# Instance normalisation on one core: transfers moved from SyncE's hardware queue to GpSimd's software queue

## The chip, the core and the metric

The kernel runs on one core of one Trainium2 chip. The core has a vector engine (VectorE, DVE in the profile), a scalar engine (ScalarE, ACT), GpSimd (POOL), SyncE (SP), a matrix engine that is not used here, and 16 DMA engines that move data between the chip's main memory and the on-chip memory SBUF. The metric is the device time in microseconds; less is better. The kernel before takes 4962.8 us, the median of five runs (4962.3 to 4964.85).

## What is computed

Every row of 4096 numbers is normalised by itself. There are 256 x 256 = 65536 rows of float32.

```
batch = 256
channels = 256
length = 4096
def reference(x: np.ndarray, eps: np.float32) -> np.ndarray:
    mean = np.mean(x, axis=2, keepdims=True)
    var = np.var(x, axis=2, keepdims=True)
    return ((x - mean) / np.sqrt(var + eps)).astype(np.float32)
```

1.07 GB are read and 1.07 GB are written.

## The kernel before

A tile is 128 partitions of 4 rows each, 512 rows or 8.39 MB; there are 128 tiles. A partition's four rows lie next to each other in memory, 64 KB in one piece. SBUF holds three such tiles, X[0] to X[2], and tile t lives in X[t % 3]; the load, the computation and the store all work in place in it.

VectorE does two passes over each row. L87 sums it (a tensor_scalar with an accumulator). ScalarE then squares the centred row with an accumulator (L137) and takes a root per pair of rows (L146). VectorE makes the reciprocal and the bias (L98, L100) and applies them (L112, a tensor_scalar without an accumulator). Of the last row of a tile, ScalarE applies the first 3072 elements (L151) and VectorE the rest.

The first and the last tile are worked in two halves of two rows each, each with its own store; the first tile is also loaded in two halves.

All transfers are issued by SyncE from one program (L196 to L218). In the middle, a loop of 41 rounds over three tiles (L208) does the same for each tile t: wait until tile t is done (L164), issue its store (L165), wait until the store of tile t-1 has landed, since tile t+2 goes into its buffer (L169), issue the load of tile t+2 (L170). The transfers of one queue start in the order of issue. So the data moves as store t, load t+2, store t+1, load t+3. At the end, after the loop has stored tile 124 and loaded tile 126, SyncE issues load 127 (L212), then store 125, store 126 and the two half stores of tile 127 (L213 to L216).

Each landing is a semaphore: loaded[s] and stored[s], one per buffer and a fourth for the second halves, each raised by 16 by one transfer. The function take (L66) waits for a value and clears the semaphore. VectorE waits for loaded itself, at the start of a tile (L85). The semaphore done[s] counts the five writes that finish a tile. GpSimd does nothing in the kernel's body.

Of the kernel before, what the change touches and what calls it, by code (L numbers as in the profile page):

```python
# [10 lines left out]
def kernel(  # L11
# [6 lines left out]
    nc = tc.nc  # L18
# [5 lines left out]
    K = 4  # L24
    BUFS = 3
# [4 lines left out]
    n, d = x_flat.shape  # L30
    assert n % (P * K) == 0 and d & (d - 1) == 0

    ntiles = n // (P * K)
    x_t = x_flat.rearrange("(t p k) d -> t p k d", p=P, k=K)
    out_t = out_flat.rearrange("(t p k) d -> t p k d", p=P, k=K)
    assert ntiles == 128

    half = K // 2
# [8 lines left out]
    X = [pool.tile([P, K, d], fp32, name=f"x{s}") for s in range(BUFS)]  # L47
# [5 lines left out]

    loaded = [nc.alloc_semaphore(f"loaded{s}") for s in range(BUFS + 1)]
    stored = [nc.alloc_semaphore(f"stored{s}") for s in range(BUFS + 1)]
    own_v = nc.alloc_semaphore("own_v")
# [3 lines left out]
    scaled = nc.alloc_semaphore("scaled")  # L62
    done = [nc.alloc_semaphore(f"done{s}") for s in range(BUFS + 1)]
    ready = nc.alloc_semaphore("ready")

    def take(engine, sem, count):  # L66
        engine.wait_ge(sem, count)  # L67
        engine.sem_clear(sem)  # L68

    V, A, S = nc.vector, nc.scalar, nc.sync  # L70

    def vector_tile(s, r0=0, k=K, ld=None, dn=None):

        x = X[s]
        ld = loaded[s] if ld is None else ld
        dn = done[s] if dn is None else dn
        own = 0

        def mine(instruction):
            nonlocal own  # L80
            own += 1
            return instruction.then_inc(own_v, 1)

        if ld:
            take(V, ld, 16)  # L85
        for r in range(r0, r0 + k):
            V.tensor_scalar(  # L87
                out=x[:, r, :], in0=x[:, r, :], scalar1=1.0 / d, scalar2=None, op0=ALU.mult, op1=ALU.add,
                accum_out=mean[s][:, r : r + 1],
            ).then_inc(means, 1)  # L90
        for b in range(r0, r0 + k, 2):
            c = slice(b, b + 2)
            final = b == r0 + k - 2
            if final:
                take(V, stds, (b - r0) // 2 + 1)
            else:
                V.wait_ge(stds, (b - r0) // 2 + 1)
            mine(V.reciprocal(out=rstd[s][:, c], in_=std[s][:, c]))  # L98
            V.wait_ge(own_v, own)
            mine(V.scalar_tensor_tensor(  # L100
                out=nbias[s][:, c], in0=mean[s][:, c], scalar=-1.0 / d, in1=rstd[s][:, c], op0=ALU.mult, op1=ALU.mult
            ))
            if final:
                take(V, own_v, own)
            else:
                V.wait_ge(own_v, own)
            if final:
                V.sem_inc(scaled, 1)
            for r in range(b, b + 2):
                c = slice(r, r + 1)  # L110
                f = slice(Q, d) if r == r0 + k - 1 else slice(0, d)
                V.tensor_scalar(  # L112
                    out=x[:, r, f], in0=x[:, r, f], scalar1=rstd[s][:, c], scalar2=nbias[s][:, c],
                    op0=ALU.mult, op1=ALU.add,
                ).then_inc(dn, 1)

    def scalar_tile(s, r0=0, k=K, ld=None, dn=None):

        x = X[s]
        dn = done[s] if dn is None else dn  # L120
        last = r0 + k - 1
        own = 0

        def mine(instruction):
            nonlocal own
            own += 1
            return instruction.then_inc(own_a, 1)

        for r in range(r0, last + 1):
            c = slice(r, r + 1)  # L130
            if own:
                A.wait_ge(own_a, own)
            if r == last:
                take(A, means, k)
            else:
                A.wait_ge(means, r - r0 + 1)
            mine(A.activation(  # L137
                out=junk, in_=x[:, r, :], func=AF.Square, bias=mean[s][:, c], scale=-float(d), accum_out=ss[s][:, c]
            ))
            if (r - r0) % 2:  # L140
                c = slice(r - 1, r + 1)
                if r == last:
                    take(A, own_a, own)
                else:
                    A.wait_ge(own_a, own)
                A.activation(  # L146
                    out=std[s][:, c], in_=ss[s][:, c], func=AF.Sqrt, bias=eps_tile, scale=1.0 / d**3
                ).then_inc(stds, 1)
        c = slice(last, last + 1)
        take(A, scaled, 1)  # L150
        A.activation(  # L151
            out=x[:, last, :Q], in_=x[:, last, :Q], func=AF.Identity, bias=nbias[s][:, c], scale=rstd[s][:, c]
        ).then_inc(dn, 1)

    def rows_of(ap, t):

        if isinstance(t, int):
            return ap[t]
        first, period, count, i = t
        ap = ap[first : first + period * (count - 1) + 1 : period]  # L160
        return ap[bass.ds(i, 1)].rearrange("o p k d -> p (o k) d")

    def store(s, t):
        take(S, done[s], K + 1)  # L164
        S.dma_start(out=rows_of(out_t, t), in_=X[s][:, :, :]).then_inc(stored[s], 16)  # L165

    def load(s, t, wait=True):
        if wait:
            take(S, stored[s], 16)  # L169
        S.dma_start(out=X[s][:, :, :], in_=rows_of(x_t, t)).then_inc(loaded[s], 16)  # L170

    def half_of(h):
        return slice(h * half, (h + 1) * half)

    def second(sems, s, h):
        return sems[BUFS] if h else sems[s]

    def store_half(s, t, h):
        r = half_of(h)
        take(S, second(done, s, h), half + 1)  # L180
        S.dma_start(out=out_t[t][:, r, :], in_=X[s][:, r, :]).then_inc(second(stored, s, h), 16)

    def halves(tile_fn, s, first):
        for h in range(2):
            ld = second(loaded, s, h) if first or h == 0 else False
            tile_fn(s, h * half, half, ld, second(done, s, h))

    last = ntiles - 1
    rounds = (ntiles - 5) // BUFS
    L0 = 2  # L190

    with tc.tile_critical():  # L192
        with nc.Block() as block:  # L193

            @block.sync
            def _(sync):  # L196
                for h in range(2):
                    r = half_of(h)
                    S.dma_start(out=X[0][:, r, :], in_=x_t[0][:, r, :]).then_inc(second(loaded, 0, h), 16)
                load(1, 1, wait=False)  # L200
                store_half(0, 0, 0)
                store_half(0, 0, 1)
                load(2, 2, wait=False)
                store(1, 1)
                take(S, stored[BUFS], 16)
                load(0, 3)

                with S.Fori(0, rounds) as i:  # L208
                    for t in range(L0, L0 + BUFS):
                        store(t % BUFS, (t, BUFS, rounds, i))  # L210
                        load((t + 2) % BUFS, (t + 2, BUFS, rounds, i))
                load(last % BUFS, last)  # L212
                store((last - 2) % BUFS, last - 2)  # L213
                store((last - 1) % BUFS, last - 1)
                store_half(last % BUFS, last, 0)
                store_half(last % BUFS, last, 1)  # L216
                for s in ((last - 2) % BUFS, (last - 1) % BUFS, last % BUFS, BUFS):
                    take(S, stored[s], 16)  # L218

            @block.vector  # L220
            def _(vector):
                V.memset(eps_tile, eps / d**2).then_inc(ready, 1)  # L222
                halves(vector_tile, 0, True)
                vector_tile(1)
                with V.Fori(0, rounds) as i:  # L225
                    for j in range(BUFS):
                        vector_tile((L0 + j) % BUFS)
                vector_tile((last - 2) % BUFS)
                vector_tile((last - 1) % BUFS)
                halves(vector_tile, last % BUFS, False)  # L230

            @block.scalar
            def _(scalar):
                take(A, ready, 1)
                halves(scalar_tile, 0, True)
                scalar_tile(1)
                with A.Fori(0, rounds) as i:
                    for j in range(BUFS):
                        scalar_tile((L0 + j) % BUFS)
                scalar_tile((last - 2) % BUFS)  # L240
                scalar_tile((last - 1) % BUFS)
                halves(scalar_tile, last % BUFS, False)
# [35 lines left out]
```

## Time and profile before

| what | value |
|---|---|
| median of five runs | 4962.8 us |
| profiled execution, its time | 4963.14 us |
| its span, first to last instruction | 4960.9 us |
| VectorE busy | 3298.2 us, 66% |
| ScalarE busy | 2407.6 us, 49% |
| L87, one row, 128x4096 | 4416 ns, 512 times |
| L112, one row, 128x4096 | 2411 ns, 382 times |
| L137, one row, 128x4096 | 3678 ns, 512 times |
| HBM read and written | 1073.74 MB each |

The span is the stretch that the profile covers; the time of the same execution has some 2.2 us more around it. Busy times are sums over instructions of one engine and may lie beside each other. In the row of 40 slices that the page has for the DMA engines each digit is the busy share of a slice in tenths. In a timeline each line has a start and a duration in microseconds, the engine, the line of the kernel, the operation and what it writes and reads; the bracket gives how long the engine was idle before it and what ended that. "SPq" is SyncE's sequencer, where transfers are issued. A DMA issue's last number is the median time from issue to landing.

### The profile page before, as it was taken

Reading aid. Unit: us, or ns where it says so; the run is one execution under the profiler, and the core shown is the slowest. Engines: PE = TensorE matmul, PEld = TensorE weight load, DVE = VectorE, ACT = ScalarE, POOL = GpSimd, SP = SyncE. Lnnn points to the kernel's source line nnn. Section 1 sums busy time; section 2 is a strip of 40 time slices with the busy share of each in tenths; the row PEclk is TensorE's granted clock in tenths of the full one; section 3 lists DMA queues with packets and bytes.
Section 4 is the critical chain, followed back from the end, with each engine's and each line's share of the span. In section 5 each row is a group of like instructions: output and inputs, shape, how many; then the busy total and the mean of one; then the engine's idle time right before and its main releaser. Section 6 shows DMA issues by size and latency. Waiting matters only on the chain.

```text
span 4960.9 us, 5954 instructions
## 1 busy us (share of the span) xinstructions
DVE 3298.2 (66%) x2049; ACT 2407.6 (49%) x1412; POOL 0.2 (0%) x4
## 2 busy tenths in 40 slices
DVE  6666666666666666666666666666666666666666
ACT  4455444554445544455445544455444554445544
POOL 0000000000000000000000000000000000000000
DMA  9999999999999999999999999999999999999999
GB/s 423 431 435 432 433 433 435 432 434 436 432 435 433 434 432 435 433 432 433 434 434 433 435 433 434 436 431 435 435 432 435 435 432 435 434 433 437 432 435 409
DMA packets 37298, 2147.52 MB, mean 433 GB/s; under 512 B 4144, under 2 KB 4144, under 8 KB 4144
## 3 DMA queue, kind: packets, MB, share of 16 engines
q1 hardware_dynamic: 37296, 2147.50, 100.0%
q14 instruction: 2, 0.02, 0.0%
HBM read 1073.74 MB, written 1073.74 MB: 433 GB/s over the span
## 4 chain that ended last, share of the span: by engine, by line
DVE 62%; another core or an unknown queue 31%; issue 4%; DMA 2%; ACT 0%; DVEq 0%; ACTq 0%; SPq 0%
DVE x L87 44%; DVE x L112 16%; DMA x<-in_x_dram 1%; DVE nbias L100 1%; DMA out_dram<-x 1%; DVE rstd L98 1%; ACT junk L137 0%; DVEq L68 0%; DVEq L225 0%; ACT L146 0%; ACT std L146 0%; DVEq L193 0%; ACTq L68 0%; ACTq L67 0%
## 5 line engine op out<-in xcount | busy, mean ns | idle before, releaser
L87 DVE TENSOR_SCALAR_CACHE_REDUCE x<-x 128x4096 f32<-128x4096 f32 x512 | 2232.3, 4416 | 1580.7 <-DMA x<-in_x_dram 1580.7
L137 ACT ACTIVATE junk<-x,mean 128x4096 f32<-128x4096 f32 x512 | 1883.1, 3678 | 2367.5 <-DVE x L87 2367.5
L112 DVE TENSOR_SCALAR x<-x,rstd,nbias 128x4096 f32<-128x4096 f32 (+1 forms) x512 | 1004.3, 2004 | 33.9 <-DVE nbias L100 29.3
L151 ACT ACTIVATE x<-x,nbias,rstd 128x3072 f32<-128x3072 f32 x130 | 383.2, 2947 | 146.3 <-DVEq L68 146.3
L137 ACT ACTIVATION_READ_ACCUMULATOR junk<-x,mean 128x1 f32 x512 | 95.5, 186 | 0.0
L146 ACT ACTIVATE std<-ss,eps_tile 128x2 f32<-128x2 f32 x256 | 75.6, 295 | 19.1
L98 DVE RECIPROCAL rstd<-std 128x2 f32<-128x2 f32 x256 | 40.8, 159 | 19.4 <-ACT std L146 19.4
L100 DVE SCALAR_TENSOR_TENSOR nbias<-mean,rstd 128x2 f32<-128x2 f32 x256 | 41.2, 161 | 8.9
L87 DVE DVE_READ_ACCUMULATOR x<-x 128x1 f32 x512 | 42.4, 83 | 0.0
L137 ACT ACT_TABLE_LOAD x1 | 1.3, 1283 | 1.2 <-DVE eps_tile L222 1.2
L146 ACT ACT_TABLE_LOAD x1 | 1.3, 1283 | 0.1
L222 DVE MEMSET eps_tile<- 128x1 f32 x1 | 0.1, 59 | 1.0 <-SPq L192 1.0
L259 POOL MEMSET const-bfloat16-1.0<- 128x1 bf16 x1 | 0.1, 101 | 0.0
L259 POOL MEMSET const-uint8-127<- 128x1 uint8 x1 | 0.1, 101 | 0.0
L259 POOL MEMSET const-float32-0.0<- 128x1 f32 x1 | 0.1, 98 | 0.2 <-issue 0.2
L259 POOL MEMSET const-float32-1.0<- 128x1 f32 x1 | 0.1, 98 | 0.0
## 6 DMA issues: line engine op xcount, KB each, us to landing
out_dram<-x SPq DMA_DIRECT2D x4, 4096.0 KB, 19.5
x<-in_x_dram SPq DMA_DIRECT2D x2, 4096.0 KB, 16.8
x<-in_x_dram SPq DMA_DIRECT2D x127, 50.3
out_dram<-x SPq DMA_DIRECT2D x126, 31.6
```

Source lines behind the costliest of these rows:

```text
L87: V.tensor_scalar(out=x[:, r, :], in0=x[:, r, :], scalar1=1.0 / d, scalar2=None, op0=ALU.mult, op1=ALU.add, accum_out=mean[s][:, r : r + 1 ...
L98: mine(V.reciprocal(out=rstd[s][:, c], in_=std[s][:, c]))
L100: mine(V.scalar_tensor_tensor(out=nbias[s][:, c], in0=mean[s][:, c], scalar=-1.0 / d, in1=rstd[s][:, c], op0=ALU.mult, op1=ALU.mult))
L112: V.tensor_scalar(out=x[:, r, f], in0=x[:, r, f], scalar1=rstd[s][:, c], scalar2=nbias[s][:, c], op0=ALU.mult, op1=ALU.add,).then_inc(dn, 1)
L137: mine(A.activation(out=junk, in_=x[:, r, :], func=AF.Square, bias=mean[s][:, c], scale=-float(d), accum_out=ss[s][:, c]))
L146: A.activation(out=std[s][:, c], in_=ss[s][:, c], func=AF.Sqrt, bias=eps_tile, scale=1.0 / d**3).then_inc(stds, 1)
L151: A.activation(out=x[:, last, :Q], in_=x[:, last, :Q], func=AF.Identity, bias=nbias[s][:, c], scale=rstd[s][:, c]).then_inc(dn, 1)
L222: V.memset(eps_tile, eps / d**2).then_inc(ready, 1)
L259: nc = _bacc.Bacc("TRN2", target_bir_lowering=False, num_devices=1)
```

## The change

All transfers are issued by GpSimd instead of SyncE, so they go to the software queue[...]. The loop is written out: 128 tiles, one after the other. VectorE doesn't wait for a load's own semaphore any more: GpSimd waits for it and raises a new semaphore, landed[0] (or landed[1] for second halves of the first tile), by one, and VectorE takes that. The semaphores loaded and stored are not cleared; they count up, and GpSimd keeps the value that is due.

The order in the middle is the same, with the new wait for the load of tile t+1 after the issue of load t+2. At the start load 2 is issued before the stores of tile 0. At the end load 127 is issued after store 125.

```diff
-    V, A, S = nc.vector, nc.scalar, nc.sync
+    V, A, S = nc.vector, nc.scalar, nc.gpsimd
...
-        if ld:
-            take(V, ld, 16)
+        if ld is not False:
+            take(V, landed[0] if ld is None else ld, 1)
...
+    due = {}
+
+    def transfer(out, in_, sem):
+        due[sem.name] = due.get(sem.name, 0) + 16
+        S.dma_start(out=out, in_=in_).then_inc(sem, 16)
+
+    def wait(sem):
+        S.wait_ge(sem, due[sem.name])
...
+    def load(t, h=None):
+        s = t % BUFS
+        r = slice(0, K) if h is None else half_of(h)
+        transfer(X[s][:, r, :], x_t[t][:, r, :], second(loaded, s, h))
+
+    def store(t, h=None):
+        s = t % BUFS
+        r = slice(0, K) if h is None else half_of(h)
+        take(S, second(done, s, h), (K if h is None else half) + 1)
+        transfer(out_t[t][:, r, :], X[s][:, r, :], second(stored, s, h))
+
+    def tell(t, h=None):
+        wait(second(loaded, t % BUFS, h))
+        S.sem_inc(landed[1] if h else landed[0], 1)
...
-            @block.sync
-            def _(sync):
...
-                with S.Fori(0, rounds) as i:
-                    for t in range(L0, L0 + BUFS):
-                        store(t % BUFS, (t, BUFS, rounds, i))
-                        load((t + 2) % BUFS, (t + 2, BUFS, rounds, i))
-                load(last % BUFS, last)
-                store((last - 2) % BUFS, last - 2)
-                store((last - 1) % BUFS, last - 1)
-                store_half(last % BUFS, last, 0)
-                store_half(last % BUFS, last, 1)
...
+            @block.gpsimd
+            def _(gpsimd):
+                load(0, 0)
+                load(0, 1)
+                load(1)
+                load(2)
+                tell(0, 0)
+                tell(0, 1)
+                store(0, 0)
+                store(0, 1)
+                tell(1)
+                for t in range(1, ntiles - 2):
+                    store(t)
+                    wait(stored[(t - 1) % BUFS])
+                    if t == 1:
+                        wait(stored[BUFS])
+                    load(t + 2)
+                    tell(t + 1)
+                store(last - 1)
+                tell(last)
+                store(last, 0)
+                store(last, 1)
+                for s in range(BUFS + 1):
+                    wait(stored[s])
```

More of the change, by code (lines that the diff above doesn't have):

```diff
@@ L64 @@
     ready = nc.alloc_semaphore("ready")
+    landed = [nc.alloc_semaphore(f"landed{h}") for h in range(2)]
     def take(engine, sem, count):
@@ L68, in take @@
         engine.sem_clear(sem)
-    V, A, S = nc.vector, nc.scalar, nc.sync
+    V, A, S = nc.vector, nc.scalar, nc.gpsimd
     def vector_tile(s, r0=0, k=K, ld=None, dn=None):
         x = X[s]
-        ld = loaded[s] if ld is None else ld
         dn = done[s] if dn is None else dn
@@ L153, in scalar_tile @@
         ).then_inc(dn, 1)
[L155 to L170, printed above, removed]
+    due = {}
[4 more added lines that the diff above has]
+        S.wait_ge(sem, due[sem.name])
     def half_of(h):
@@ L176, in second @@
         return sems[BUFS] if h else sems[s]
[L178 to L181, printed above, removed]
+    def load(t, h=None):
[10 more added lines that the diff above has]
+        S.sem_inc(landed[1] if h else landed[0], 1)
     def halves(tile_fn, s, first):
         for h in range(2):
-            ld = second(loaded, s, h) if first or h == 0 else False
+            ld = landed[h] if first or h == 0 else False
             tile_fn(s, h * half, half, ld, second(done, s, h))
@@ L193 @@
         with nc.Block() as block:
-            @block.sync
-            def _(sync):
[L197 to L206, printed above, removed]
-                with S.Fori(0, rounds) as i:
-                    for t in range(L0, L0 + BUFS):
-                        store(t % BUFS, (t, BUFS, rounds, i))
-                        load((t + 2) % BUFS, (t + 2, BUFS, rounds, i))
-                load(last % BUFS, last)
-                store((last - 2) % BUFS, last - 2)
-                store((last - 1) % BUFS, last - 1)
-                store_half(last % BUFS, last, 0)
-                store_half(last % BUFS, last, 1)
-                for s in ((last - 2) % BUFS, (last - 1) % BUFS, last % BUFS, BUFS):
-                    take(S, stored[s], 16)
+            @block.gpsimd
[22 more added lines that the diff above has]
+                    wait(stored[s])
             @block.vector
```

## The prediction

> **What bounds the kernel now.** I read the page first: busy row, the row of DMA shares, the queue rows, the DMA issues. Then the waits, the timeline of one tile in the middle, and the timeline of the end; and the landing events and packet records of the trace for single times.
>
> ```profile
> span 4960.9 us, 5954 instructions
> DVE 3298.2 (66%) x2049; ACT 2407.6 (49%) x1412; POOL 0.2 (0%) x4
> DMA  9999999999999999999999999999999999999999
> DMA packets 37298, 2147.52 MB, mean 433 GB/s; under 512 B 4144, under 2 KB 4144, under 8 KB 4144
> q1 hardware_dynamic: 37296, 2147.50, 100.0%
> ...
> out_dram<-x SPq DMA_DIRECT2D x4, 4096.0 KB, 19.5
> x<-in_x_dram SPq DMA_DIRECT2D x2, 4096.0 KB, 16.8
> x<-in_x_dram SPq DMA_DIRECT2D x127, 50.3
> out_dram<-x SPq DMA_DIRECT2D x126, 31.6
> ```
>
> The 16 DMA engines are full in every slice, DVE idles for a third. One tile is 8.39 MB each way, 19.3 us at 434 GB/s; load plus store is 38.6 us, and 128 of these are 4945 us of the 4960.9. The median store lands 31.6 us after its issue, of which 19.3 is its own movement: it stands in the queue for 12.3 us before its turn. That is the slack of the middle. The waits say the same from DVE's side, and the timeline of a middle tile shows it:
>
> ```profile
> DVE x L87 <- DMA x<-in_x_dram: 1580.7, 126, 13.9
> ```
>
> ```profile
> 2434.28 0.34 SPq L165 DMA_DIRECT2D out_dram<-x  x1
> 2434.86 0.35 SPq L170 DMA_DIRECT2D x<-in_x_dram  x1
> 2446.50 4.42 DVE L87 TENSOR_SCALAR_CACHE_REDUCE x<-x 128x4096 f32<-128x4096 f32 x1 [12.46 <-DMA x<-in_x_dram]
> ```
>
> Tile t is done and both its store and the load of t+2 are issued at 2434.9; the load in progress lands only at 2446.4. DVE does nothing in those 12 us.
>
> At the end the last tile's two half stores are still covered by work queued ahead of them:
>
> ```profile
> 4882.17 4.42 DVE L87 TENSOR_SCALAR_CACHE_REDUCE x<-x 128x4096 f32<-128x4096 f32 x1 [12.64 <-DMA x<-in_x_dram]
> ...
> 4908.16 4.41 DVE L87 TENSOR_SCALAR_CACHE_REDUCE x<-x 128x4096 f32<-128x4096 f32 x1
> ...
> 4925.21 17.21 SPq L181 DMA_DIRECT2D out_dram<-x  x2
> ```
>
> Tile 126 lands at 4882.0 and starts at 4882.17; tile 127 starts at 4908.16 without a wait, so it had landed (4901.4 by the trace's landing events). Its half stores go out at 4925.21 and 4942.1 (25.21+17.21 less one issue of 0.34); the last landing is 4959.6, and the span ends 1.4 later.
>
> **What the Trainium skill says.** (1) "DMA: Bandwidth & Descriptors", The descriptor swizzle: a software transfer over 128 partitions makes 9 read and 9 write descriptors per engine, 8 of data and one of completion. The hardware queue here has the same cut: 259 transfers x 16 x 9 = 37296 packets, the very count of the profile's page. (2) Same page, Specifications: first byte about 1 us on the software path, about 0.6 on the hardware one. Here the first issue is at 0.96 and the first data packets start at 2.0, so 1.0 on the hardware path; the software path is not in this trace. (3) "SBUF — State Buffer", Who interferes with whom: a tensor_scalar that doesn't write its accumulator can take both SBUF ports and shuts GpSimd out from writing descriptors until it ends. The trace agrees as to which form is the fast one: L112 takes 2411 ns for 4096 elements, L87 with accumulator 4416. No run here shows the shutting out. (4) Same DMA page, Anatomy of one DMA: the software path fits 2.0 us + bytes/436e3, so its steady rate equals what I see here (434 GB/s).
>
> **The change part by part.** Sums stand against the profiled execution: span 4960.9, time 4963.14, 2.2 us around it; the median of the runs is 4962.8, so I carry the difference over to that.
>
> *Middle, 123 tiles.* Order on the queue: store t, load t+2, as before. New on POOL: a wait for the landing of t+1 and a semaphore increment before the next store. Queued behind that wait is only store t+1, which needs tile t+1 computed and so landed anyway: no cost. The relay puts perhaps 0.1 to 0.3 us (two semaphore steps; DVE here starts 0.15 us after a landing) before DVE's start, and the store's descriptors are later by the software path's delay. Both come out of the 12.3 us slack. Even 3 us per issue would fit. DVE's fast form runs in the microseconds before done, and DVE is idle from done to the next landing, just where both issues fall; so the lock of (3) has nothing to hold up. Cost 0 while issue to first byte stays under some 12 us; past that each microsecond costs 126.
>
> *Rate of the stream.* The trace's packet records give 2418 ns for 65536 bytes and 1213 for 32768: 1205 ns per 32 KB and 8 ns fixed per packet. Each engine moves 2048 rows, 2048 x 2418 = 4952 us: the whole span. So 1 ns more per row is 2 us. By (1) and (4) I take the same packets and the same rate: 0. Bounds: below, all 8 ns fixed gone, -16.4; above, rows cut in two +16.4, in four +49, in sixteen +246 (8 ns for each extra piece).
>
> *Head.* Before: first issue 0.96, first bytes 2.0. POOL does four memsets by 0.44 and starts with the block like SP. Taken +0.8 (skill: +0.4; up to 3 for the first software issue). Load 2 now stands before the stores of tile 0: the same bytes in another order; four issues stand before the first tell, and half 0's landing at 12.7 leaves them 11 us. Tile 2 is told only after load 3 is issued, which waits for the stores of tile 0 (landing 62.4+19.3 = 81.7). Then landing-to-issue as in the middle (2407.7 to 2434.3, 26.6) gives its store at 108.5, its turn is at about 120: 0.
>
> *Tail.* This is a part of the diff that isn't about the queue. Before: load 127 was queued ahead of store 125. After: store 125, load 127, store 126, halves. The bytes are the same, but load 127 lands one store later: 4901.4+19.4 = 4920.8. DVE starts at 4920.8+0.15+0.2 = 4921.1, 12.95 later than 4908.16. The half stores go out at 4938.2 and 4942.1+12.95 = 4955.05. The queue ends store 126 at 4940.2 and the first half at 4949.9: the first half is just in time, the second finds the engines dry for 5 us. An issue to empty engines lands after 12.1 us (the least of the page's load halves, 0.96 to 13.1), with the software path 12.9: 4968.0, against 4959.6. So +8.4. Bounds: +7.6 with no software delay, +11 with 3 us of it (the first half late too).
>
> *Instruction fetch.* POOL's program is unrolled over 125 tiles instead of looped: some 80 KB instead of the 20 KB of queue q14, at 27 GB/s of one engine 2 to 3 us on that engine if all fall on one. The engines end 6.4 us apart (4953.2 to 4959.6 in the last landing), so only the slowest counts. Taken +0.8, bounds 0 to 3.
>
> *End.* POOL waits for the four stored semaphores as SP did: 0, bound +2 for closing the software queue.
>
> Sum: 0.8 + 8.4 + 0.8 = +10.0, and about 1 for the unknown closing: 4962.8 + 11 = 4974.
>
> **The rivals.** A change under 0.2% (9.9 us) can't be told from none here.
> A, forecast: the middle and the rate as before, head and tail as above, +8 to +17; 4974, own range 4969 to 4982. For it: 12.3 us slack, same packet cut. Against: no software transfer is in the trace.
> B: the software ring costs per row, by smaller pieces or by one engine that the ring slows down. 4974+16 = 4990 for one cut, 5023 for four pieces, 5220 for sixteen. For it: a saturated stream hides nothing. Against: the page's 9 descriptors and 436 GB/s.
> C: generation is slower than the slack, for instance held up by DVE. At 15 us it is 3 x 126 = 380 us, 5350. Against it: DVE idle at both issues.
> D, other side: not slower. The software ring has less fixed time per row than 8 ns; from about 5 ns less (10 us) the tail is paid back, with all 8 gone 4974-16 = 4958. For it only that the fixed part exists; against, that 32768 bytes in 1205 ns is the engine's own pace and leaves just these 8.
>
> **How the numbers follow.** A 0.62, of which the low end of its costs (tail 7.6, head 0.4, nothing else) stays within 0.2%: 0.33 slower, 0.29 same. B 0.24, all slower. C 0.06, slower. D 0.08: same 0.05, faster 0.03. Slower 0.63, same 0.34, faster 0.03. The time is A's. The range 4967 to 5024 takes in A's lower end and B up to four pieces, and leaves out C, the most of D and B beyond it: about 0.18.
>
> **What would show it.** A: packets of POOL's queue again 37296, DMA full in the middle slices, stores landing about 31 us after issue, a DVE idle of about 12 us per tile less the relay, a dry stretch near the end with the last half store landing 12 to 14 us after its issue. B: more packets or fewer GB/s in the middle. C: DVE waits well above 1580 us and stores landing near 20 us after issue. Wrong altogether if tile 127 starts before store 125 is through, or if the span shrinks with the middle's GB/s unchanged.

## The result and the profile after

The changed kernel takes 4973.09 us, the median of 25 runs (4972.45 to 4975.45, and one run of 5018.53 that the last section comes back to); the kernel before took 4962.9 us beside it (45 runs). The ratio is 1.0024, with a 95% interval of 1.0018 to 1.0030: slower by 10.2 us. The forecast was 4974 us, range 4967 to 5024.

The profiled execution of the changed kernel has a time of 4972.7 us and a span of 4970.9. First the lines of its page: busy times, DMA share by slice, GB/s by slice, packets, queue, and the DMA issues with the median time to landing.

```profile
span 4970.9 us, 5378 instructions
DVE 3298.3 (66%) x2049; ACT 2407.7 (48%) x1412; POOL 136.9 (3%) x263
...
DMA  9999999999999999999999999999999999999998
GB/s 421 430 436 431 434 433 433 435 432 436 432 437 432 437 432 437 432 436 433 434 435 433 435 433 436 433 436 432 437 432 436 432 435 434 435 434 432 437 432 371
DMA packets 37302, 2147.55 MB, mean 432 GB/s; under 512 B 4144, under 2 KB 4144, under 8 KB 4144
q0 software_dynamic: 37296, 2147.50, 99.8%
...
out_dram<-x POOLq DMA_DIRECT2D x4, 4096.0 KB, 22.2
x<-in_x_dram POOLq DMA_DIRECT2D x2, 4096.0 KB, 17.0
x<-in_x_dram POOLq DMA_DIRECT2D x127, 49.9
out_dram<-x POOLq DMA_DIRECT2D x126, 31.1
```

The queue has changed and the packets have not: again 37296. Every slice but the last is as full as before; the last falls to 371 GB/s, and its digit to 8. The median store still lands 31.1 us after its issue. One tile in the middle, from the timeline (start and duration in us, engine, line, operation; L88 and L113 are the L87 and L112 of before, and L160 is the one line that issues all transfers):

```profile
2434.58 0.53 POOL L160 DMA_DIRECT2D out_dram<-x  x1 [37.69 <-DVE x L113]
2435.10 0.53 POOL L160 DMA_DIRECT2D x<-in_x_dram  x1
2446.45 4.42 DVE L88 TENSOR_SCALAR_CACHE_REDUCE x<-x 128x4096 f32<-128x4096 f32 x1 [12.46 <-POOLq L184]
```

The moments are those of before to a fraction of a microsecond (before in brackets): store issued at 2434.58 (2434.28), DVE's next start at 2446.45 (2446.50), idle 12.46 in both. What ended the idle time is now the relay on GpSimd (L184) and no longer the DMA. An issue takes GpSimd 0.53 us. The middle gives nothing and takes nothing.

The end, from the timeline and from stretches of two microseconds (engine asked for, its busy time and instructions, granted clock, share of the DMA engines, GB/s):

```profile
4920.44 4.42 DVE L88 TENSOR_SCALAR_CACHE_REDUCE x<-x 128x4096 f32<-128x4096 f32 x1 [12.64 <-POOLq L184]
...
4938.00 0.53 POOL L160 DMA_DIRECT2D out_dram<-x  x1 [29.07 <-DVE x L113]
...
4954.88 0.53 POOL L160 DMA_DIRECT2D out_dram<-x  x1 [16.35 <-DVE x L113]
```

```profile
4946.00:4948.00 2.00, 0.00 (x0) 1.00 1.22 524
4948.00:4950.00 2.00, 0.00 (x0) 1.00 0.00 0
4950.00:4952.00 2.00, 0.00 (x0) 1.00 0.00 0
4952.00:4954.00 2.00, 0.00 (x0) 1.00 0.00 0
4954.00:4956.00 2.00, 0.53 (x1) 1.00 0.19 82
4956.00:4958.00 2.00, 0.00 (x0) 1.00 1.04 442
```

Tile 127 starts at 4920.44 after a wait; before it started at 4908.16 without one. The first half store has landed at 4949.39 (landing events), the second is issued at 4954.88, and in between no DMA engine moves anything. It lands at 4966.24; before, the last landing was at 4959.58. Then comes something that the kernel before doesn't have, in the instructions of the line that closes the block (duration min/median/max in ns, first and last start in us). DRAIN is the instruction that stands there ahead of an engine's last semaphore events. GpSimd's in the changed kernel:

```profile
L196 POOLq DRAIN  x1: 3087/3087/3087, 4966.5 to 4966.5; - x1
```

SyncE's in the kernel before:

```profile
L193 SPq DRAIN  x1: 7/7/7, 4959.7 to 4959.7; - x1
```

GpSimd's drain at its end takes 3.09 us; SyncE's in its place took 7 ns. From last landing to the span's end are 4.7 us, before 1.4. So 10.0 us more of span are 6.7 us of later last landing and 3.3 of closing. At the start DVE's first row is 0.9 us later (14.17, before 13.26), but the stream has made that up by the end: the transfer ahead of store 126 lands at 4920.25, before at 4920.77.

### The profile page after: what moved, and what is told of

Its sections match the earlier page's. It is cut to its first block, busy times and chain, and to the rows that moved or that the text cites. A ratio compares the mean times of both kernels' runs of the same rounds, so it can differ in the third digit from the quotient of the medians.

```text
span 4970.9 us, 5378 instructions
## 1 busy us (share of the span) xinstructions
DVE 3298.3 (66%) x2049; ACT 2407.7 (48%) x1412; POOL 136.9 (3%) x263
## 3 DMA queue, kind: packets, MB, share of 16 engines
q0 software_dynamic: 37296, 2147.50, 99.8%
## 4 chain that ended last, share of the span: by engine, by line
DMA 56%; DVE 36%; another core or an unknown queue 4%; issue 3%; POOL 1%; ACT 0%; POOLq 0%; DVEq 0%; ACTq 0%; PEldq 0%
DMA x<-in_x_dram 55%; DVE x L88 25%; DVE x L113 9%; POOL out_dram L160 1%; DMA out_dram<-x 1%; DVE nbias L101 1%; DVE rstd L99 0%; ACT junk L138 0%; POOL x L160 0%; POOLq L184 0%; DVEq L70 0%; POOLq L70 0%; ACT std L147 0%; DVEq L229 0%
## 5 line engine op out<-in xcount | busy, mean ns | idle before, releaser
L88 DVE TENSOR_SCALAR_CACHE_REDUCE x<-x 128x4096 f32<-128x4096 f32 x512 | 2232.4, 4416 | 1592.8 <-POOLq L184 1592.8
L113 DVE TENSOR_SCALAR x<-x,rstd,nbias 128x4096 f32<-128x4096 f32 (+1 forms) x512 | 1004.2, 2004 | 33.9 <-DVE nbias L101 29.3
L160 POOL DMA_DIRECT2D out_dram<-x x130 | 69.1, 531 | 4805.6 <-DVE x L113 4805.6
L160 POOL DMA_DIRECT2D x<-in_x_dram x129 | 68.8, 533 | 12.6 <-DMA out_dram<-x 6.2
L88 DVE DVE_READ_ACCUMULATOR x<-x 128x1 f32 x512 | 42.4, 83 | 0.0
## 6 DMA issues: line engine op xcount, KB each, us to landing
out_dram<-x POOLq DMA_DIRECT2D x126, 31.1
```

The source lines that it names most:

```text
L88: V.tensor_scalar(out=x[:, r, :], in0=x[:, r, :], scalar1=1.0 / d, scalar2=None, op0=ALU.mult, op1=ALU.add, accum_out=mean[s][:, r : r + 1 ...
L113: V.tensor_scalar(out=x[:, r, f], in0=x[:, r, f], scalar1=rstd[s][:, c], scalar2=nbias[s][:, c], op0=ALU.mult, op1=ALU.add,).then_inc(dn, 1)
L160: S.dma_start(out=out, in_=in_).then_inc(sem, 16)
```

## The experiments

**The order at the end, alone and with the rest.** The changed program has three parts: another queue, a written out loop with a relay, another order at the end. Four runs take them apart. e1 is the changed kernel on SyncE:

```diff
-    V, A, S = nc.vector, nc.scalar, nc.gpsimd
+    V, A, S = nc.vector, nc.scalar, nc.sync
```

> The changed kernel's program word for word (loop written out, relay, load 127 after store 125) issued by SyncE on the hardware queue. Theory, order: the last half store still finds dry engines, goes out near 4955 us and lands 11.5 to 12 us later, and the end costs 1.4 us: span 4967 to 4969, time +6 to +7 over before (about 4969.5). Rival, queue: head, software issue and closing make the whole +10, so with the hardware queue the time is back within 2 us of before (4963 to 4965).

e2 keeps GpSimd and puts load 127 ahead of store 125 again:

```diff
-                for t in range(1, ntiles - 2):
+                for t in range(1, ntiles - 3):
...
+                wait(stored[(last - 3) % BUFS])
+                load(last)
+                store(last - 2)
+                tell(last - 1)
                 store(last - 1)
```

> The changed kernel with load 127 issued ahead of store 125 as in the kernel before; all on GpSimd. Theory, order: no dry stretch at the end, last landing 4959 to 4961 us, then 4.7 us of closing: span about 4964.5, time about 4966 (+3 to +4 over before). Rival, queue: the software queue makes it all, time stays at 4973.

e5 is the kernel before, looped and on SyncE, with only that exchange:

```diff
-                load(last % BUFS, last)
                 store((last - 2) % BUFS, last - 2)
+                load(last % BUFS, last)
```

> The kernel before, looped and on SyncE, with two lines exchanged: store 125 issued ahead of load 127. Theory, order: the exchange alone makes a dry stretch before the last half store; last landing about 4967, span about 4968, time +6 to +8 over before (4969 to 4971). Rival: the +10.7 of the whole program on SyncE comes from its being written out and relayed, then the exchange alone is worth less than 3 (below 4966).

e6 is e2's program on SyncE:

> The changed program on SyncE's hardware queue with load 127 ahead of store 125 as before: written out and relayed, but no new order at the end. Theory, order plus a lagging engine: the engine that fell behind by 4 us in the run on SyncE does it here too, time +3 to +4 (4966 to 4967). Rival: the lag was of that one profile, time within 1.5 of before (4962 to 4964.5), and the exchange is worth the full 10 in the written out program.

Medians in us, with the ratio to the kernel before in the same session (4962.9):

| | old order at the end | new order at the end | the order |
|---|---|---|---|
| SyncE, looped | before, 4962.9 | e5, 4969.3 (1.0006 to 1.0020) | +6.4 |
| SyncE, written out, relay | e6, 4966.0 (0.9999 to 1.0016) | e1, 4973.6 (1.0014 to 1.0029) | +7.6 |
| GpSimd, written out, relay | e2, 4965.8 (0.9997 to 1.0014) | changed kernel, 4973.1 | +7.3 |

Read across, the exchange costs 6.4 to 7.6 us on either queue. e5's timeline shows it in the old program:

```profile
4922.33 4.42 DVE L87 TENSOR_SCALAR_CACHE_REDUCE x<-x 128x4096 f32<-128x4096 f32 x1 [12.62 <-DMA x<-in_x_dram]
...
4939.38 17.21 SPq L181 DMA_DIRECT2D out_dram<-x  x2
```

Tile 127 starts late behind a wait of 12.62 us, and the second half store goes out at 4956.3, after the engines have gone dry. Read down, the queue and the written out program together are worth some 3 us, and their intervals reach 1.0. The last two rows differ in the queue alone, and there it moves nothing that can be told from none: 4966.0 and 4965.8 with the old order, 4973.6 and 4973.1 with the new. e1 was 4 us above its expectation, so e6 was added: with the old order the written out program on SyncE is 3.1 above before, as its first theory had it. In the profiles of e1 and e6 one DMA engine falls ever further behind the others in the second half of the run: at the load of tile 127 the last of the 16 landing events is 3.4 us after the one before it in e1 (4924.58 and 4921.22), 1.2 in the changed kernel. What slows that engine isn't settled; on SyncE it costs about what the drain costs on GpSimd. Writing out and relay were not taken apart.

**The closing.** e7 repeats e2, whose first profile fell on a run of 5013.4 us:

> The same kernel as e2_pool_old_end, for a profile of its usual time (its first profile has 5013 us). Theory: last landing near 4959.5, then GpSimd's drain of about 3 us, span near 4964; packets longer than their usual 2418 ns appear only in the first 1000 us. Rival: the drain is short when the last store followed a full queue.

It took 4965.1 us; last landing at 4958.66 us, earlier than before's 4959.58, and then the drain, from the same view as above:

```profile
L196 POOLq DRAIN  x1: 3087/3087/3087, 4958.9 to 4958.9; - x1
```

e3 asks whether that is the price of any use of the software queue. To the kernel before it adds one transfer on GpSimd:

```diff
+            @block.gpsimd
+            def _(gpsimd):
+                nc.gpsimd.dma_start(out=touch[:, :], in_=x_flat[0:P, 0:128]).then_inc(touched, 16)
+                nc.gpsimd.wait_ge(touched, 16)
```

> The kernel before plus one transfer of 64 KB that GpSimd issues at the start, waits for, and nobody uses. Theory, closing is a fixed price of having used the software queue at all: GpSimd's drain at its end takes about 3 us instead of 0.04; here GpSimd reaches its end while the stream runs, so the price is hidden and the time is within 1 us of before. Rival, the 3.09 us drain depends on what stands in the queue at that moment (259 transfers, or one just landed): the drain is far below 3 us here. Either way the time moves by less than 1 us plus the 64 KB itself (0.15 us).

4962.85 us, ratio 0.9990 to 1.0007: no change. Its drain:

```profile
L195 POOLq DRAIN  x1: 125/125/125, 8.7 to 8.7; - x1
```

125 ns after one transfer, 3087 after 259, and 5211 in the two runs below with 384. A run of the same 259 transfers that lasts 5630 us has 3087 again. So the fixed price fell: the drain is longer the more transfers GpSimd has issued, and it doesn't depend on the time, nor on the up to 750 pad clearings that GpSimd does in the runs below (3087 again). It is not proportional: some 11.5 ns for each transfer from 1 to 259, 17 for each of the next 125. Whether transfers or their packets count, these runs do not tell apart.

**How much lateness the middle hides.** e4 lets GpSimd clear a pad twice between done and the store's issue, e8 once, in 125 tiles (d, from the start of the first clearing to the issue, is what the profile shows: 5.9 and 3.2 us; against the changed kernel the issue comes 5.5 and 2.7 us later):

```diff
+        for _ in range(late):
+            S.memset(pad, 0.0).then_inc(padded, 1)
+            take(S, padded, 1)
         transfer(out_t[t][:, r, :], X[s][:, r, :], second(stored, s, h))
```

> The changed kernel with GpSimd clearing a pad of 128x3000 twice between done and the issue of the store, in 125 tiles; delay d of some 6 us as the profile will show. Theory, slack: the middle has 12 us (store issue to the landing of the load ahead of it, less 1.4 to the first byte: about 10.3 to spare), so the time stays within 3 us of the changed kernel, and stores land d sooner after their issue (31.1 less d). Rival, no slack: each late issue is paid, 125 x d = +700 us or so.

> One pad clearing ahead of each store in place of two: d about 3.0 us. Theory, spread: the engines run up to 7.8 us apart, so the foremost one has only 11.7 - 7.8 - 1.4 = 2.5 us of room, and once a late store holds it back the engines run in step, where packets stretch at each change from loads to stores; at 3.0 us a small part of them is held back: between 0 and +25 us over the changed kernel. Rival, one slack for all engines of 10.3 us: within 2 us of the changed kernel. Rival, GpSimd's clearing itself slows the stream whatever the slack: +29 us, half of the +58 of two clearings.

Both theories of e4 missed. It took 5031.2 us (1.0122 to 1.0153): +58 over the changed kernel, neither 0 nor 700. e8's six runs fall in two groups: 4974.4 and 4975.8, and four from 5021.5 to 5026.4. That is neither a part of e4's loss nor half of it: it is all or nearly nothing, at the same work of GpSimd, so GpSimd's clearing as such is not what slows the stream. The rate by slice shows where e4 loses, line of its page:

```profile
GB/s 409 432 433 431 427 431 428 432 427 431 427 426 433 426 432 426 426 433 426 432 426 432 427 426 432 426 430 429 429 430 425 432 426 425 433 426 426 433 425 369
```

Slices of 425 to 427 come all through the run, where the changed kernel has 430 or more in all but the first and the last. The trace's packet records tell what a slow slice is made of. Of 32384 packets of 64 KB nearly all take 2418 ns; those over 2500 are counted here, with their excess over 2418 summed and divided by the 16 engines. The last two columns are from the landing events, as medians between 1000 and 4500 us: the spread from first to last of the 16 landings of one transfer, and the room of the first engine, which is the time from the issue of a store to the first of the 16 landings of the load ahead of it.

```
profile of              over 2500 ns   excess per engine   time over its usual   spread   room
before                           290              5.8 us                     -   4.8 us   7.5 us
changed kernel                   114              3.4 us                     -   6.5 us   5.3 us
e7 (e2 again)                    189              3.5 us                     -   6.5 us   5.2 us
e8, its run of 4975.8            433              7.9 us                     -   4.2 us   4.9 us
e2, its run of 5013.4           1442             46.9 us   47.6 (over 4965.8)   10.1 us   2.1 us
e4, its run of 5032.7           2329             60.2 us   59.6 (over 4973.1)    4.7 us   1.8 us
```

The stretched packets are most of the lost time: less the 3.5 and 3.4 us of the usual runs, 43.4 of 47.6 us and 56.8 of 59.6. In the changed kernel and in e7 they come in the first 1000 us and then all but cease, while the 16 engines drift apart; before has half of its 290 later, the last at 2366 us. In e4 and in e2's long run they never cease.

How far the engines lie apart doesn't tell the long runs from the usual ones: in e4 the drift stops at some 4.7 us, with 13 of 16 landings within 0.6 us of the first, but in e2's long run it goes on to 10.1, past the 6.5 of e7, which is the same kernel. What the long runs share is the first engine's room. It is about 5 us or more in the usual runs and about 2 in the long ones, near the 1.4 us from an issue to its first packets. In e2's long run it falls from 10 us at the start to 2.3 just after 1000 us, and the stretching sets in there. In e1 it shrinks from 6.9 to 2 us as one engine lags, and 118 of its 292 stretched packets come after 4500 us. A late store shortens the time from its issue to the load's last landing (11.8 us in the changed kernel, 9.0 in e8, 6.8 in e4), and the foremost engine's slack is that less the spread: e8's run of 4975.8 keeps its room because its spread is only 4.2. A short room is not all of it, since packets are stretched in the first 250 us of every run too, where the room of the usual runs is still about 8 to 11 us and the spread on average 1.2 to 1.7. What stretches the packets, and why the drift of one kernel stops in one run and goes on in another, no run shows.

**Past all slack.** e9 has six clearings, d 16.9 us; e10 the same without the relay, VectorE waiting for the load's own semaphore:

```diff
-            take(V, landed[0] if ld is None else ld, 1)
+            V.wait_ge(*ld)
...
-                    tell(t + 1)
```

> Six pad clearings ahead of each store: d about 16.3 us, past the slack. Theory, relay in line: GpSimd tells of tile t+1 only after it has issued store t and load t+2, so a tile takes 1.25 (issue to DVE's start) + 26.5 (DVE's start to done) + 16.3 = 44.0 us instead of 38.64: +5.4 x 124 = +670, about 5640. Rival, the price on record (125 or 126 us for each us past 12): +4.3 x 126 = +540, about 5515.

> The same delay, but VectorE waits for a load's own semaphore (its program written out, counting up), GpSimd relays nothing. Theory: a late store then holds up every second tile only: two tiles take 1.4 + 38.7 + 1 (store and load to the landing) + 26.7 + 16.3 = 84 us instead of 77.3, +3.4 per tile, +420, about 5390; up to +470 with stretched packets. Rival, the price on record: +540 here as well.

e9 took 5630 us, +657 over the changed kernel, and e10 5442, +468 (one run each): the two prices differ by far more than the 60 us of the long runs above, as the theory said. The timeline of e9, the late store, the load, DVE's start, and the next late store:

```profile
2417.13 0.53 POOL L162 DMA_DIRECT2D out_dram<-x  x1 [0.59 <-POOL pad L183]
2417.75 0.54 POOL L162 DMA_DIRECT2D x<-in_x_dram  x1
2417.90 4.42 DVE L90 TENSOR_SCALAR_CACHE_REDUCE x<-x 128x4096 f32<-128x4096 f32 x1 [17.83 <-POOLq L189]
...
2461.05 0.53 POOL L162 DMA_DIRECT2D out_dram<-x  x1 [0.60 <-POOL pad L183]
```

DVE has been idle 17.83 us and starts as soon as GpSimd has issued its two transfers: the relay stands in line behind them. The period is 43.92 us, expected 44.0. In e10, the same view:

```profile
2462.72 4.42 DVE L90 TENSOR_SCALAR_CACHE_REDUCE x<-x 128x4096 f32<-128x4096 f32 x1 [14.37 <-DMA x<-in_x_dram]
2465.40 0.53 POOL L162 DMA_DIRECT2D out_dram<-x  x1 [0.59 <-POOL pad L183]
```

Here DVE starts on a landing, 2.7 us ahead of GpSimd's issue. The stores go out 44.2 and 40.6 us apart in turn: only every second tile is held up, 84.6 us for two where the theory has 84.

**The port lock.** e11 issues the middle tiles' stores in two halves, the first while VectorE is about to run its fast form; e12 clears a small pad first, so that the issue falls inside it:

```diff
+    def store_two(t):
+        s = t % BUFS
+        S.wait_ge(done[s], half)
+        S.memset(pad, 0.0).then_inc(padded, 1)
+        take(S, padded, 1)
+        transfer(out_t[t][:, half_of(0), :], X[s][:, half_of(0), :], stored[s])
+        take(S, done[s], K + 1)
+        transfer(out_t[t][:, half_of(1), :], X[s][:, half_of(1), :], stored[s])
```

(the lines with the pad are e12's alone)

> The middle tiles' stores in two halves, the first issued when rows 0 and 1 are done, while VectorE runs its fast form (L113) on row 2. Theory, port lock as the skill states: GpSimd's issue of the first half takes longer than its usual 0.53 us in most tiles, up to about 3 us, since its descriptors wait for VectorE. Rival: the issue stays at 0.53 us, no lock is seen. The time stays within 10 us of the changed kernel in both.

> As e11_store_in_two_parts, with a pad of 128x700 cleared ahead of the first half's store, so that its issue falls inside VectorE's fast form on row 2 (L113 begins 0.15 us after the old issue). Theory, port lock: the issue of the first half lasts until VectorE's instruction ends, some 1.5 to 3 us in most tiles in place of 0.53. Rival, no lock on this path: 0.53 us. In both the time stays near e11's 5029, since the second half's issue is not held up by more than 2 us.

In e11 the issues stay at 533 ns, but they begin 0.15 to 0.29 us ahead of L113, which was not the case to be tried. In e12, where L115 is that same line, the timeline shows it:

```profile
2416.43 3.15 DVE L115 TENSOR_SCALAR x<-x,rstd,nbias 128x4096 f32<-128x4096 f32 x2 [0.18 <-DVE nbias L103]
2417.31 1.68 POOL L162 DMA_DIRECT2D out_dram<-x  x1 [0.58 <-POOL pad L187]
2420.17 0.53 POOL L162 DMA_DIRECT2D out_dram<-x  x1 [1.18 <-DVE x L115]
```

The first half's issue begins 0.9 us after L115 and takes 1.68 us instead of 0.53; it ends at 2418.99, just after the first of the two rows (2416.43 + 2.41 = 2418.84). The second issue, after VectorE is through, takes 0.53. So it is in all 125 tiles: the issue begins 0.45 to 1.07 us into VectorE's instruction, takes 1461 to 2081 ns and ends 0.12 us after that instruction does. The lock that the Trainium skill describes in "SBUF — State Buffer", Who interferes with whom, is seen here. The times missed: e11 took 5028.8 us (1.0114 to 1.0148) and not within 10 us of the changed kernel, e12 5034.6 in one run, inside e11's range (5025.9 to 5035.3), so the lock adds no time that can be seen. In e11 too most of the loss is stretched packets: 49.3 us per engine counted as above, half stores included (4.1 in the changed kernel), of the 62.2 that its profiled run of 5035.3 is longer. Another 8 are the fixed 8 ns of 1000 more packets per engine, and 2.1 the longer drain. Its stores are issued sooner, not later, and still the first engine's room at the first half is 2.2 us (3.3 in e12, where the issue takes longer): a late store is not the only way there.

## Why the prediction was right, step by step

- **Middle at no cost, same packets, same rate** (rival B against it): right. 37296 packets, idle of 12.46 us per tile in both, GB/s as before.
- **Order at the end**: right in mechanism, and the largest term. DVE's start was forecast at 4921.1 and came at 4920.44, the last issue 4955.05 and 4954.88. The term that was too large is issue to landing on empty engines: 12.9 us in the forecast, 11.4 measured (11.1 on SyncE's queue in e1 and e5, where the forecast took 12.1 from the first load). The last landing was forecast 9.2 us later with the head's shift (8.4 + 0.8), and was 6.7: 1.5 of the difference is this latency, 0.8 the head. The term's lower bound of 7.6 was broken.
- **Head**, +0.8: measured +0.9 at the first landing, made up before the end. The 0.4 us that the Trainium skill has between the two paths ("DMA: Bandwidth & Descriptors", Specifications) is near, its values of about 1 and 0.6 are not: issue to first data packets is 1.4 us here (1.49 to 2.86), on the hardware queue 1.0.
- **Closing**, about +1 with a bound of +2: too small. The drain alone is 3.09 us; closing is +3.3. This bound was broken too.
- **Instruction fetch**, +0.8: not seen. Four more fetch packets of 8 KB (queue q14) at 309 ns each, instead of 60 KB more.

With the instruction fetch the last landing was forecast 3.3 us too late, and the closing 2.3 too short. The two errors nearly cancel: that the total of 11 comes so near to 10.2 is luck, while the largest term's mechanism is not.

Two statements beside the forecast were wrong. The slack was given as 12.3 us, with 3 us per issue fitting well inside; that is the last engine's, the first one has 5.3, and e8 loses 50 us in four of six runs at 3.2. And rival C's price of 126 for each microsecond past the slack gave +540 for e9, where it was +657: issues 16.5 us later cost 5.3 us per tile (657 / 125), which the price has only with a slack of 11.2. One delay was tried past the slack, so the price per microsecond isn't shown. e10 shows that the relay makes much of it: without the relay the same delay costs 3.7 us per tile. The reason why C did not come, DVE idle at both issues, stands: no issue of the changed kernel overlaps L113, and in e12 an overlap makes the issue some 1.1 us longer.

No run beats the kernel before; e3 equals it. Rivals B, C and D had no part.

## What to carry to other kernels

Split a change into queue, program and order before giving its cost to the queue: here an exchange of two transfers at the end costs 6.4 us by itself, while the queue alone, in one and the same program, changes less than 1 us: its closing of 3.1 us stands against an engine that lags on the other queue. A stream that fills the engines in the middle still goes dry where the last tile's computation has no transfer left ahead of it, so look at the last two loads first. The slack of an issue is that of the foremost DMA engine, so read the first of the 16 landings and not the last; and a relay on the issuing engine stands in line behind its issues.

## What had not been expected

The drain at the end of GpSimd's program is longer the more transfers it has issued: 125 ns for 1, 3087 for 259, 5211 for 384. And this stream of loads and stores has two paces: 434 GB/s while each store is issued some 5 us or more before the foremost engine is through with the load ahead of it, and about 1% less where that room is about 2 us, with packets of 64 KB that take up to 4.3 us instead of 2.42. One run of the changed kernel in 25 (5018.53 us) and the first of e2 (5013.4) were that much longer with nothing changed; for e2 the packets show it, for the changed kernel that run has no profile here. What tips a run one way or the other stays open.
